# Raw first projections for two blocks, and the first block of x over two queues, in a two-layer convolutional decoder on eight cores

## The chip, the cores and the metric

One Trainium2 chip, 8 NeuronCores, one program launched on all of them. The metric is the device time in microseconds (us) of the slowest core. A program on all eight cores has a second, slower state in some executions, in which one die runs at a lower granted clock; only runs in the fast state are compared here. "Mean core span" below is the mean over the eight cores and over the fast runs of a kernel of the time from a core's first to its last instruction. It scatters less than the time, which one late core decides.

Engines: PE (TensorE), DVE (VectorE), ACT (ScalarE), POOL (GpSimd) and SP (SyncE, which issues loads). A **projection** in this text, as in the prediction, is one matmul of 128x128 weights by 128x512 (or 128x64) tokens; eight of them, one for each chunk k of the 1024 channels, make one output tile.

## The reference, cut to what matters

```python
def hybrid_layer(x, ...):                       # two layers
    h = rmsnorm(x, norm_g)                      # x * rsqrt(mean(x^2) + eps) * g
    p = h @ w_in                                # a, gate, z_A | B, C, hb, z_B
    u = a_val * sigmoid(a_gate);  v = gc * hb   # GLU; gated product
    ca = layernorm(causal_dwconv(u, ...))       # width 31, group A
    y_a = silu(ca) * silu(z_a)
    y_b = gb * causal_dwconv(v, ...) * silu(z_b)    # width 3, group B
    return x + concat(y_a, y_b) @ w_out
```

Each core has 2048 + 64 tokens, in four blocks of 512 and one of 64 (blocks 0 to 4).

## The kernel before: the parts that matter here

The kernel is written as a list of operations with their dependencies. Its own scheduler, a Python class that runs when the program is built, plays the operations through with assumed durations and load times, and thereby fixes the order of the instructions on every engine. Each engine then works its list off in that order, with semaphore waits.

```python
class Sched:
    def op(self, eng, fn, dur, reads=(), writes=(), chan=None, dma=0.0, pkt=0.1, lat=0.0, ..., urgent=False, name=""): ...
    def run(self):          # plays all ops; an op starts when its inputs are there BY THE ASSUMED TIMES
        ...                 # -> self.order[engine], the instruction order
    def emit(self, ...):    # puts out each engine's list in that order, with the waits it needs
```

The RMS statistic of a block: four pairs of squares on ACT, added in pairs on DVE, then one matmul with ones for each pair (a "statistic"), then Ln and Exp, then h = x * gain * rstd on DVE. (The last pair of block 0 goes to PE unsummed, as two matmuls.) While block 0's statistics come in, both kernels also put out **filling matmuls** of 128 columns ("warm" in the source), whose result nobody reads: 62 before, 60 after.

```python
def rms_stat(part, ...):
    for kp in range(4):
        act(Square, x[2kp], x[2kp+1] -> s)                      # 128x1024
        dve(s[:n] += s[n:2n])                                   # pair sum
        mm("stat", b, n, [(ones, s[:n])], urgent=True, ...)     # one 512-column matmul
    lo = act(Ln, b -> r);  ex = act(Exp(-0.5 * r) -> b)
def rms_apply(...): dve(h[k] = x[k] * gain[k] * b)              # eight times
```

The start: x of block 0 in four loads of 512 KB on the SP queue, the gain vector ("vecs", 28 KB) on the ACT queue, everything else on the POOL queue, in the order below. w1 to w4 are the weight slices of group A's first heads, w5 and w6 those of group B.

```python
    x_load(0)                                                      # SP, four loads
    S.op("act", dma vecs <- vecs_d, chan="c0", dma=0.2, pkt=0.02)  # gain vector
    ...                                                            # POOL: five memsets, then
    wA = [w_load(8), w_load(0), w_load(9), w_load(1)]              # w1..w4
    x_load(1, ("pool",))
    wB = [w_load(32), w_load(40)]                                  # w5, w6
    for q in (2, 3, 4): x_load(q, ("pool",))
```

## Time and profile before

| | before |
|---|---|
| time, fast runs | 1117.88 and 1116.79 us (a third run, 1326.98, was slow) |
| spans of the cores, profiled execution (1121.72 us) | 1113.4 to 1116.3 us, core 6 1120.2 |
| first projection, mean of the cores | 16.85 us |
| w5 lands, mean | 27.90 us |
| "mark" (first projection with weights from y_sb), mean | 83.70 us |
| span minus mark | 1031.0 to 1031.2 us on seven cores |

The rows read: until the mark the start decides, after it PE runs nearly without waits for 1031 us. The lines of the profile are shown in the prediction.

### The profile page before, as it was taken

To read this page: it belongs to the slowest core of one execution; us is meant where nothing else is said; L and a number is where in the kernel's file an instruction comes from. 1 tells how busy PE (TensorE), PEld (TensorE's weight loads), DVE (VectorE), ACT (ScalarE), POOL (GpSimd) and SP (SyncE) were. 2 spreads that over 40 slices of the span, in tenths; PEclk is the share of its full clock that TensorE was granted. 3 is DMA by queue.
4 is the path that set the end of the run, shared out by engine and by line. 5 is a ranking of instruction groups with operands and counts; after the bars stand their busy time and mean duration, and the time that the engine had idled before them with its cause. 6 is when DMAs were issued, how large, how long until landed. Compare 5 with 4: busy or idle time off the path is not lost.

```text
span 1120.2 us, 20967 instructions; the slowest of 8 cores (1113.4 to 1120.2 us)
## 1 busy us (share of the span) xinstructions
PE 1093.2 (98%) x7087; PEld 545.4 (49%) x7087; DVE 762.7 (68%) x1583; ACT 442.6 (40%) x705; POOL 254.6 (23%) x409
## 2 busy tenths in 40 slices
PE   5999899999999999999999999999999999999996
PEld 3445455454545455444444545545454454554545
DVE  3675756886785777744774577587668668874667
ACT  4652334234431435542442144342533134553354
POOL 7212222131201211113471112102211021110162
PEclk9999999999999999999999999999999999999998
DMA  9947488546643666651033746936655247565025
GB/s 219 237 79 139 66 149 152 110 82 108 117 80 51 121 110 113 95 128 20 1 40 57 162 97 112 178 72 121 114 97 94 49 92 130 91 99 121 2 104 207
DMA packets 178824, 117.98 MB, mean 105 GB/s; under 512 B 139168, under 2 KB 152352, under 8 KB 178656
## 3 DMA queue, kind: packets, MB, share of 16 engines
q0 software_dynamic: 34352, 54.97, 31.6%
q1 hardware_dynamic: 144224, 61.65, 22.4%
q8 instruction: 59, 0.97, 0.4%
q14 instruction: 45, 0.37, 0.1%
q10 hardware_dynamic: 144, 0.03, 0.0%
HBM read 132.24 MB, written 36.19 MB: 150 GB/s over the span
## 4 chain that ended last, share of the span: by engine, by line
PE 95%; DMA 1%; DVE 1%; POOL 1%; ACT 1%; issue 0%; DVEq 0%; ACTq 0%; POOLq 0%
PE psb L617 91%; PE psb L797 2%; PE psb L799 2%; DMA wsl<-w_in_r 1%; DVE x_sb L720 0%; POOL toep L1015 0%; ACT L694 0%; POOL wsl L584 0%; POOL x_sb L984 0%; POOL u_sb L1004 0%; DVE h_sb L720 0%; ACT L736 0%; ACT psb L700 0%; ACT tmp L694 0%; POOL up_sb L1013 0%
## 5 line engine op out<-in xcount | busy, mean ns | idle before, releaser
L617 PE MATMUL psb<-h_sb,wsl 128*128 128x512 bf16 (+1 forms) x4160 | 762.7, 343 | 4.6 <-DMA wsl<-w_in_r 2.6
L617 PEld LDWEIGHTS psb<-h_sb,wsl 128*128 128x128 bf16 x4160 | 347.2, 98 | 382.5 <-issue 11.6
L617 PE MATMUL psb<-y_sb,wsl 128*128 128x512 bf16 (+2 forms) x992 | 186.9, 336 | 0.2 <-DVE x_sb L943 0.2
L943 DVE TENSOR_TENSOR x_sb<-x_sb,psb 128x512 f32<-128x512 f32 (+2 forms) x248 | 137.3, 577 | 50.6 <-PE psb L617 49.4
L617 PEld LDWEIGHTS psb<-y_sb,wsl 128*128 128x128 bf16 x992 | 85.1, 98 | 87.2 <-issue 0.3
L584 POOL DMA_DIRECT2D wsl<-w_in_r x104 | 56.0, 546 | 287.0 <-PE psb L617 205.6
L924 DVE SCALAR_TENSOR_TENSOR tmp<-vbuf,cw_b_sb,tmp 128x512 f32<-128x512 bf16 (+1 forms) x160 | 102.9, 654 | 15.7 <-ACT tmp L921 6.9
L738 DVE SCALAR_TENSOR_TENSOR u_sb<-tmp,psb 128x512 bf16<-128x512 f32 (+1 forms) x80 | 47.3, 592 | 76.3 <-PE psb L617 68.4
L736 ACT ACTIVATE tmp<-psb 128x512 f32<-128x512 f32 (+1 forms) x80 | 41.3, 521 | 138.5 <-PE psb L617 121.3
L892 ACT ACTIVATE tmp<-psb 128x512 f32<-128x512 f32 (+1 forms) x80 | 41.4, 520 | 136.0 <-PE psb L617 131.5
L894 DVE TENSOR_TENSOR vbuf<-psb,tmp 128x512 bf16<-128x512 f32 (+1 forms) x80 | 47.3, 594 | 61.2 <-PE psb L617 57.9
L775 DVE COPY toep<-wt_sb 32x512 bf16<-32x512 bf16 x256 | 75.2, 295 | 18.8 <-DMA wt_sb<-wt_d 7.2
L675 ACT ACTIVATE tmp<-x_sb 128x1024 bf16<-128x1024 f32 (+2 forms) x63 | 52.3, 856 | 69.1 <-DVE x_sb L943 58.6
L804 DVE TENSOR_TENSOR big<-psb,cbt_sb 128x320 bf16<-128x320 f32 x128 | 62.4, 487 | 23.4 <-PE psb L799 18.6
L769 POOL DMA_DIRECT2D wt_sb<-wt_d x64 | 34.8, 545 | 187.2 <-DVE toep L775 94.5
L929 ACT ACTIVATE tmp<-psb 128x512 f32<-128x512 f32 (+1 forms) x80 | 41.0, 521 | 88.6 <-PE psb L617 79.9
L883 ACT ACTIVATE tmp<-psb 128x512 f32<-128x512 f32 (+1 forms) x80 | 40.1, 521 | 70.2 <-PE psb L617 66.2
L921 ACT ACTIVATE tmp<-vbuf,cw_b_sb 128x512 f32<-128x512 bf16 (+1 forms) x80 | 50.5, 642 | 42.0 <-DVE vbuf L894 38.8
L878 ACT ACTIVATE tmp<-big,vecs_sb 128x512 f32<-128x512 bf16 (+1 forms) x80 | 54.4, 729 | 31.7 <-DMA big<-scr_c 31.3
L720 DVE SCALAR_TENSOR_TENSOR h_sb<-x_sb,vecs_sb,psb 128x512 bf16<-128x512 f32 (+1 forms) x80 | 47.3, 648 | 17.4 <-ACT psb L700 17.4
L617 PE MATMUL psb<-h_sb,y_sb 128*128 128x512 bf16 (+1 forms) x320 | 58.9, 342 | 0.0
L931 DVE TENSOR_TENSOR tmp<-psb,tmp 128x512 f32<-128x512 f32 (+1 forms) x80 | 46.7, 594 | 17.5 <-PE psb L617 13.8
(80 smaller groups left out, 941.4 us busy)
## 6 DMA issues: line engine op xcount, KB each, us to landing
wsl<-w_in_r POOLq DMA_DIRECT2D x104, 256.0 KB, 5.9
scr_u<-u_sb SPq DMA_DIRECT2D x16, 768.0 KB, 6.2
up_sb<-scr_u SPq DMA_DIRECT2D x16, 768.0 KB, 6.4
scr_c<-big SPq DMA_DIRECT2D x16, 640.0 KB, 6.6
big<-scr_c SPq DMA_DIRECT2D x16, 640.0 KB, 5.1
wt_sb<-wt_d POOLq DMA_DIRECT2D x64, 128.0 KB, 3.7
x_sb<-x_d POOLq DMA_DIRECT2D x12, 512.0 KB, 20.2
wsl<-w_out_r POOLq DMA_DIRECT2D x24, 256.0 KB, 5.3
```

The source lines that it names most:

```text
L584: return e.dma_start(out=wsl[:, v.slot, :], in_=src)
L617: ins = e.matmul(bank(v, n), lhsT=l_(), rhs=r_(), start=(first and i == 0), stop=(last and i == len(pairs) - 1))
L675: act((lambda e, s=s, kp=kp: e.activation(out=tmph[:, s.slot, 0:2 * n].rearrange("p (k c) -> p k c", k=2), in_=x2(kp, part), func=AF.Square)),
L720: dve((lambda e, k=k, out=out: e.scalar_tensor_tensor(out=out, in0=xs(k, part), scalar=vecs[:, gcol0 + k:gcol0 + k + 1], in1=bank(r, n), o ...
L738: dve((lambda e: e.scalar_tensor_tensor(out=u_blk(ub, q), in0=b3(tm(th, n), q), scalar=1.0, in1=b3(bank(bv, n), q), op0=ALU.add, op1=ALU.m ...
L775: dve((lambda e, p=p, c=c: e.tensor_copy(toep[p, tp.slot, :].rearrange("p (m x) -> p m x", x=128)[:, :, 32 * c:32 * c + 32], wt_sb[p, w.sl ...
L804: dve((lambda e, b=b, v=v, bias=bias: e.tensor_tensor(out=big[:, co.slot, 4 * b:4 * b + 4, :], in0=banks[v.slot][:, 0:384].rearrange("p (g ...
L878: act((lambda e, s=s, q=q, n=n: e.activation(out=b3(tm(s, n), q), in_=c_blk(cn.slot, q), func=AF.Silu, scale=vecs[:, 16 + col:17 + col], b ...
L894: dve((lambda e: e.tensor_tensor(out=v_blk(q, 0), in0=b3(bank(bh, n), q), in1=b3(tm(th, n), q), op=ALU.mult)), n, [bh, th], [v_r[q]], name ...
L921: act((lambda e, a=a, q=q, n=n: e.activation(out=b3(tm(a, n), q), in_=v_blk(q, 0), func=AF.Copy, scale=cw_b[:, l, j, 2:3])), n, [v_r[q], c ...
L924: dve((lambda e, a=a, q=q, n=n, lag=lag: e.scalar_tensor_tensor(out=b3(tm(a, n), q), in0=v_blk(q, lag), scalar=cw_b[:, l, j, 2 - lag:3 - l ...
L943: dve((lambda e: e.tensor_tensor(out=xs(m, part), in0=xs(m, part), in1=bank(v, n), op=ALU.add)), n, [v, xr], [xr], name=f"x{q}.{m}")
```

## The change

Intent: blocks 0 and 1 are projected from x * gain, without waiting for the RMS statistic; the scale by token (rstd) is multiplied into the result in PSUM afterwards. h itself, which later heads need, is made later on ACT and POOL ("finishing"). Squares of blocks 0 to 3 go to PE without a pair sum, so a pair takes two statistic matmuls in place of one. x of block 0 is issued by SP and ACT in turn. The heads are interleaved a little differently, and the slack for loads is 3.5 in place of 4.25.

```diff
 ORDER = [
-    "b0 C0 Z0 P2 a1 b1 C1 P3 C2 P4 Z1 O4 ...
+    "C0 b0 Z0 P2 a1 b1 C1 P3 P4 Z1 C2 O4 ...
+DIRECT = (0, 1, 2, 3)
+START = "u0 u1 h0 t0 t1 w0 w1 w2 w3 x1 w4 w5 x2 x3 x4"
+RAW = (0, 1);  FINISH = {2: (0,), 3: (1,)};  WARM = (20, 20, 20, 0)
-SLACK, SLACK_DMA, SLACK_FIRST, QUIET = 1.5, 4.25, 2.0, 40.0
+SLACK, SLACK_DMA, SLACK_FIRST, QUIET = 1.5, 3.5, 2.0, 40.0
 def rms_stat(...):
+    if direct:                                  # both squares straight to PE
+        st = mm("stat", b, n, [(ones, s[i*n:(i+1)*n]) for i in range(2)], ..., urgent=True)
+        continue
+def raw_scale(q):  dve(h[k] = x[k] * gain[k])                        # eight times
+def raw_finish(q, rv):  act(t = x[k] * gain[k]);  pool(h[k] = t * rv)    # eight times each
 def p1_block(..., rv=None):
+    dve(psum_g *= rv);  ...  dve(psum_v *= rv)                       # if raw
 def pb_a_block(..., rv=None):
-    act(copy c)
+    act(copy c)  or, if raw,  dve(c = psum_c * rv^2)
-x_load(0)
+x_load(0, ("sp", "act"))                        # the gain vector is issued behind x
 S.op("act", dma vecs <- vecs_d, chan="c0", dma=0.2, pkt=0.02)
```
(cut to its core)

## The prediction

> **What bounds the kernel now.** I first read the spans of the cores. Seven of the eight take 1113.4 to 1116.3 us; core 6, which the page shows, takes 1120.2. No die is slower than the other, so this is the fast state. The page's busy times and TensorE's waits on core 6 come next:
>
> ```profile
> PE 1093.2 (98%) x7087; PEld 545.4 (49%) x7087; DVE 762.7 (68%) x1583; ACT 442.6 (40%) x705; POOL 254.6 (23%) x409
> PE psb L617 <- DVE tmp L677: 10.5, 7, 6.6
> PE psb L617 <- DVE big L819: 3.2, 1, 3.2
> PE psb L617 <- DMA wsl<-w_in_r: 2.6, 1, 2.6
> PE psb L617 <- DVE h_sb L720: 2.0, 3, 0.9
> ```
>
> TensorE (PE) is the bound. It waits 18.5 us in all, and the waits restricted to the first 60 us hold nearly all of it. The 6.6 us piece ends at 6.63 us, before any projection exists. The 3.2 us wait (at 127.5 to 130.7 us) is on core 6 alone: none of the other seven lists it. So only the start can give time. The chain of waits over the start of core 6 (start, us, what):
>
> ```profile
> 3.79 3.49 POOL toep L1015 x2
> 7.28 2.26 POOL wsl L584 x4
> 9.54 2.04 POOL x_sb L984 x4
> 11.58 16.61 DMA wsl<-w_in_r
> 28.32 14.16 PE psb L617 x58
> ```
>
> The chain hardly sees the RMSNorm of block 0. It runs through GpSimd's issue of loads and through one load: the fifth weight slice ("w5", first of group B), issued at 11.58 us and landed at 28.2. To see how far this sets the end I took the first projection that reads its weights from y_sb as a mark: by then the same 256 wide and 64 narrow projections are done on each core.
>
> ```profile
> L617 PE MATMUL psb<-h_sb,y_sb x320: 192/379/382, 82.2 to 652.0; 128*128 128x512 bf16 x128, 128*128 128x64 bf16 x32
> L617 PE MATMUL psb<-h_sb,y_sb x320: 192/379/382, 84.1 to 658.8; 128*128 128x512 bf16 x128, 128*128 128x64 bf16 x32
> ```
>
> These are cores 0 and 6: marks 82.2 and 84.1. In order of cores 0 to 7 the marks are 82.2, 85.0, 83.0, 85.1, 82.5, 84.8, 84.1, 83.0, and w5 (11.58 us plus its time to landing) lands at 26.8, 28.9, 27.3, 27.8, 27.4, 28.7, 28.2, 28.1. Mark minus w5 is 54.9 to 57.3, mean 55.8 us. Span minus mark is 1031.0 to 1031.2 us on seven cores (1036.1 on core 6, with its extra wait). So the kernel is **w5's landing (26.8 to 28.9) + 55.8 + 1031.2**, and the last term is PE at full pace. A time lies some 1.5 us over the slowest span (1121.72 for 1120.2); 1116.3 + 1.5 gives 1117.8, as in the fast runs.
>
> The last view is the clock, in stretches of 5 us on core 6:
>
> ```profile
> 25.00:30.00 5.00, 2.44 (x8) 0.75 (x9) 1.19 (x3) 4.10 (x6) 5.00 (x10) 0.79 1.02 254
> 30.00:35.00 5.00, 5.00 (x22) 2.07 (x21) 2.80 (x6) 2.92 (x5) 1.28 (x3) 0.87 0.99 344
> ```
>
> The last three columns are granted clock, DMA share, GB/s. The clock drops after the wait for w5, and the DMA engines are full. The missing clock times 5 us is 1.7 us on core 6, 3.4 on core 3, nothing on cores 4 and 7.
>
> **What the Trainium skill says.** (1) "TensorE: Matmul & The Clock Gate", Part 1: after an idle window of about 3.4 us the clock is halved until PE has been busy for one. The trace agrees: weight loads 0.43 us apart from 28.3 to 31.3 us, 0.216 later. (2) "DMA: Bandwidth & Descriptors", "Issuing engines are not separate DMA queues": loads from several engines share 16 DMA engines, a second issuer saves only issue time. The trace agrees so far: four x loads take 1.81 us to issue, but land at about 4.8, 7.4, 9.8 and 11.0, with the DMA share at 0.98 from 5 to 10 us. (3) "GPSIMD Engine Reference", Key points: GpSimd shares its SBUF interfaces with VectorE and contends with its two-port modes. No row here isolates it. (4) "ScalarE: Activation LUTs", "What ACT_TABLE_LOAD costs": 1283 ns per load; the trace has 1283.
>
> **The change part by part.** I count with the instruction order of both programs.
>
> *Raw block 0.* Projections no longer wait for squares, sum, Ln, Exp (h from 15.64 us, first projection at 16.65). They need a piece of x times the gain, one VectorE tensor-by-scalar (0.42 us for 128x512 f32, from the like row at L1043), and weights. But w1 to w4 land on core 6 at 13.2, 15.3, 16.7 and 18.6 (issue plus landing), and the new order asks for w1, w2, w3 at its first three projections and for w4 at the seventh. So PE starts 3 us sooner and does six projections by 18.6. Then come 26 of block 0, the first of block 1 and the statistics of block 1, paced by x of block 1 (20.4 to 24.4 us, plus a square of 1.06). All of this ends near 26.5, and the next projection waits for w5.
>
> *What is done when w5 lands.* Before: 30 projections. After: 34, plus all of block 1's statistics. That is the point: four projections, 4 x 0.2166 = 0.9 us, not the 3 us of the earlier start. (0.2166 is 41 projections from 31.26 to 40.14.)
>
> *From w5 to the mark.* Before: 226 wide projections and 9 wide statistics x 0.2166 = 50.9, plus 68 narrow x 0.029 = 2.0: 52.9; measured 55.8, so 2.9 us of waits and half clock. After, statistics feed both squares straight to PE, twice the matmuls: 222 + 16 = 238 x 0.2166 = 51.5 + 2.0 = 53.5. Block 1 has no rms chain in front of its projections, and block 2's (x landed 35.8 us, h estimated from 40) comes before PE needs it (28.2 + 70 x 0.2166 = 43.4). So the waits of 0.87 and 0.40 us on h should go. I leave 0.9 us for half clock on the slower cores: 54.4. Gain **1.4 us**.
>
> *Two queues for x.* The bytes ahead of w5 are the same and the DMA engines full. I allow w5 **0.5 us** sooner.
>
> *ScalarE, GpSimd, VectorE.* Added: 16 scaled copies on ScalarE x 0.72 (L712) = 11.5 us, 16 products on GpSimd x 1.30 (L717) = 20.9, and on VectorE 16 raw scalings x 0.42 = 6.7 and ten PSUM products (five a raw block) x 0.69 (L894) = 6.9. Gone from VectorE: 16 h products x 0.74 (L720) = 11.9 and 15 pair sums x 0.43 = 6.5, so it comes out 4.8 lighter. The finished h of block 0 is needed at the 184th projection (w5 + 149 x 0.2166 + 3.5 = about 63.5 us), of block 1 at the 217th (about 73). GpSimd can start at about 35 us, so 20.9 us end well before, if ScalarE (26.5 us busy of 40 between 30 and 70 us) makes room for 11.5 more.
>
> *Reordered heads, smaller DMA slack.* No saving: after the mark PE already runs without waits. Sum: -1.4 - 0.5 = about -1.9 us on a fast time of 1117.3.
>
> **The rivals.** *The start pays in full.* If x lands clearly sooner over two queues, weights and w5 follow by 2 us and more, and with block 1 raw some 4 us go: near 1113. For: x moves at only some 250 GB/s then, against 330 later. Against: engines already 0.98 busy. *A new wait behind the finishing work.* ScalarE at 38 of 40 us may hold up tanh or Ln, or GpSimd's products the halo copy, the next weight loads and the first convolution: PE would wait 2 to 5 us, time 1118 to 1121. Against: seven of eight cores have 5 us and more between the halo data's landing (91 on core 0) and its use. *Nothing,* if w5 lands as late and half clock stays: about 1117. *The new order after the mark* could bring waits such as core 6's 3.2 us, for one core is enough to set the time.
>
> **Range and chances.** Centre 1115.5 us (1117.3 - 1.9, rounded). Low 1111 holds the first rival with a lucky set of cores, high 1119 the second one at half strength. Two per cent would be 22 us, more than all the waits of PE together, so I give faster 0.01, within 2% 0.97, slower 0.02 (a wait in every round of heads).
>
> **What would show it right or wrong.** Right: the first projection near 13 to 14 us, a wait on w5 near 27 us still in PE's waits, the h waits gone, mark at w5 + 54 to 55, span minus mark again 1031. Wrong: w5 landing under 26 us (two queues help), mark minus w5 over 56 (new waits on VectorE, ScalarE or GpSimd rows of the finishing work), or span minus mark over 1033 (the reorder costs).

## The result, and the profile after

| | before | after | after, again |
|---|---|---|---|
| time, median | 1117.8 us (fast runs 1116.79 to 1117.88) | 1119.41 us (1118.25 to 1121.27) | 1120.12 us (fast runs 1117.98 to 1121.40) |
| ratio to before, 95% interval | | 1.0019 [0.9999, 1.0039] | 1.0013 [1.0001, 1.0026] |
| first projection, mean of the cores | 16.85 | 15.47 | 15.79 |
| w5 lands, mean | 27.90 | 27.26 | 26.99 |
| projections and wide statistics done when w5 lands, mean | 29.8 and 8.0 | 31.9 and 14.4 | 30.5 and 13.9 |
| mark, mean | 83.70 | 83.88 | 83.93 |
| span minus mark, undisturbed cores | 1031.2 | 1031.4 to 1031.6 | 1031.5 to 1031.6 |

A ratio is the mean time of one kernel's fast runs over that of the other's of the same rounds, so it is not quite the ratio of the medians. The prediction was 1115.5 us with a range of 1111 to 1119: the class (within 2%) was right, the time lies a little above the range and the sign of the small change is wrong. Counts of instructions by a point of time are taken from the trace's records, of which a few are missing.

The page of the changed kernel shows a span of 1116.8 us and nothing odd at this scale:

```profile
PE 1093.7 (98%) x7100; PEld 545.1 (49%) x7100; DVE 764.4 (68%) x1577; ACT 451.9 (40%) x719; POOL 275.9 (25%) x425
```

The added work on ACT (+9.3 us) and POOL (+21.3 us) is where it was expected; DVE has 1.7 us more in place of the 4.8 us less that the prediction gave (the page before was core 6, this is core 4). What PE waited for on core 6, the core that the prediction read (us in total, times, longest):

```profile
PE psb L623 <- ACT tmp L670: 9.7, 2, 8.7
PE psb L623 <- DMA wsl<-w_in_r: 2.0, 2, 1.6
PE psb L623 <- DVE tmp L678: 1.4, 2, 0.9
PE psb L623 <- DVE tmp L933: 0.7, 1, 0.7
```

The 8.7 us piece lies before any projection, as the 6.6 us piece did before. The 1.4 us for L678 lie after the mark. The waits on h are gone, as predicted (on seven of eight cores; core 3 has 0.26 and 0.54 us). New is 0.98 us for a square of block 2 (L670) and 0.7 us for the product that takes the place of a copy (L933). And the weight wait has another meaning: it is no longer for w5, but for w3 (1.63 us) and w4 (0.39 us), just after the first projections. The chain of waits of that core (start, us, what) says the same from the other end:

```profile
9.54 2.10 POOL x_sb L1025 x4
11.64 0.97 POOL wsl L590 x2
12.61 18.91 DMA x_sb<-x_d
...
31.60 1.06 ACT tmp L670
...
33.72 0.70 DVE tmp L933
```

Before, the long load in this chain was w5; now it is x of block 2 (issued at 12.61 us), then its square, then the product. So it is on cores 1, 2, 3 and 6, where the first square of block 2 starts 0.1 us after its x has landed. On cores 0, 4, 5 and 7 it starts 0.3 to 0.9 us after, straight behind a copy of the finishing work (L735). ScalarE on core 5, where that x landed at 30.50 us:

```profile
30.47 0.71 ACT L735 ACTIVATE big<-x_sb,vecs_sb 128x512 f32<-128x512 f32 x1
31.08 1.04 ACT L670 ACTIVATE tmp<-x_sb 128x1024 bf16<-128x1024 f32 x1
```

PE waits for this square for 0.60 to 0.61 us on these four cores, and for 0.96 to 1.12 us on the other four.

The marks answer to the two lines of the prediction for cores 0 and 6 (fourth figure; 311 of 320 records are there):

```profile
L623 PE MATMUL psb<-h_sb,y_sb x311: 193/379/382, 83.0 to 652.8; 128*128 128x512 bf16 x124, 128*128 128x64 bf16 x32
L623 PE MATMUL psb<-h_sb,y_sb x311: 192/379/382, 84.2 to 654.2; 128*128 128x512 bf16 x124, 128*128 128x64 bf16 x32
```

Core 0 went from 82.2 to 83.0, core 6 from 84.1 to 84.2. Finally the stretches of 5 us from 25 and 30 us on core 6 (PE, weight loads, DVE, ACT, POOL; then clock, DMA share, GB/s):

```profile
25.00:30.00 5.00, 5.00 (x25) 2.28 (x24) 2.74 (x6) 2.49 (x4) 3.91 (x8) 1.00 1.07 272
30.00:35.00 5.00, 3.23 (x15) 1.17 (x15) 1.98 (x4) 4.61 (x7) 3.49 (x6) 1.00 0.98 316
```

From 25 to 30 us PE gained, from 8 instructions to 25: the wait for w5 is gone. From 30 to 35 it lost, from 22 to 15. **The wait moved; it did not go.**

### The profile page after: what moved, and what is told of

Its sections match the earlier page's. It is cut to its first block, busy times and chain, and to the rows that moved or that the text cites. A ratio compares the mean times of both kernels' runs of the same rounds, so it can differ in the third digit from the quotient of the medians.

```text
span 1116.8 us, 21060 instructions; the slowest of 8 cores (1114.2 to 1116.8 us)
## 1 busy us (share of the span) xinstructions
PE 1093.7 (98%) x7100; PEld 545.1 (49%) x7100; DVE 764.4 (68%) x1577; ACT 451.9 (40%) x719; POOL 275.9 (25%) x425
## 4 chain that ended last, share of the span: by engine, by line
PE 96%; DMA 2%; POOL 1%; DVE 0%; ACT 0%; issue 0%; DVEq 0%; ACTq 0%; POOLq 0%
PE psb L623 92%; DMA x_sb<-x_d 2%; PE psb L835 2%; PE psb L837 2%; DVE x_sb L752 0%; POOL toep L1060 0%; POOL wsl L590 0%; POOL x_sb L1025 0%; POOL u_sb L1056 0%; ACT tmp L670 0%; POOL up_sb L1058 0%; DVE tmp L678 0%; DVEq L1159 0%; DVE x_sb L984 0%; DVEq L413 0%
## 5 line engine op out<-in xcount | busy, mean ns | idle before, releaser
L931 ACT ACTIVATE tmp<-psb 128x512 f32<-128x512 f32 (+1 forms) x78 | 40.2, 518 | 135.2 <-PE psb L623 131.5
L813 DVE COPY toep<-wt_sb 32x512 bf16<-32x512 bf16 x256 | 77.9, 305 | 15.9 <-DMA wt_sb<-wt_d 3.0
L769 ACT ACTIVATE tmp<-psb 128x512 f32<-128x512 f32 (+1 forms) x76 | 38.7, 517 | 114.3 <-PE psb L623 100.4
L970 ACT ACTIVATE tmp<-psb 128x512 f32<-128x512 f32 (+1 forms) x80 | 41.2, 521 | 104.1 <-PE psb L623 81.9
L670 ACT ACTIVATE tmp<-x_sb 128x1024 bf16<-128x1024 f32 (+2 forms) x64 | 53.5, 859 | 72.5 <-DVE x_sb L984 58.2
L962 ACT ACTIVATE tmp<-vbuf,cw_b_sb 128x512 f32<-128x512 bf16 (+1 forms) x80 | 50.4, 642 | 58.0 <-DVE vbuf L935 54.4
L921 ACT ACTIVATE tmp<-psb 128x512 f32<-128x512 f32 (+1 forms) x80 | 40.7, 521 | 74.8 <-PE psb L623 65.0
L922 DVE TENSOR_TENSOR y_sb<-tmp 128x512 bf16<-128x512 f32 (+1 forms) x70 | 41.2, 599 | 25.5 <-ACT tmp L921 25.0
```

The source lines that it names most:

```text
L670: act((lambda e, s=s, kp=kp: e.activation(out=tmph[:, s.slot, 0:2 * n].rearrange("p (k c) -> p k c", k=2), in_=x2(kp, part), func=AF.Square)),
L813: dve((lambda e, p=p, c=c: e.tensor_copy(toep[p, tp.slot, :].rearrange("p (m x) -> p m x", x=128)[:, :, 32 * c:32 * c + 32], wt_sb[p, w.sl ...
L962: act((lambda e, a=a, q=q, n=n: e.activation(out=b3(tm(a, n), q), in_=v_blk(q, 0), func=AF.Copy, scale=cw_b[:, l, j, 2:3])), n, [v_r[q], c ...
```

## The experiments

Eighteen runs were made. The figures of those that recur are in the table at the end of this section; the texts before it give the edit and what follows. "Core span +0.65" means the mean core span of the kernel minus that of the kernel before in the same call; the kernel before gave 1114.44 to 1114.80 in the five calls, so differences under 0.4 us say little. A mark comes from one profiled execution; four profiles with the same order at the start (the changed kernel twice, f1 and e3) have marks of 83.21 to 83.93.

### Is there a difference at all, and what does one part do?

**a0, the changed kernel again.** No edit.

> The changed kernel once more, unedited, in more rounds. It measures the size of the difference to be explained and how much start and mark differ between executions. If the change costs what the first timing said, the fast runs give a ratio of 1.001 to 1.003 (1118.5 to 1120.5 us). If that was chance, the interval holds 0.998, the 1115.5 us that were predicted. Mean mark of the cores 83.5 to 84.3 us, span minus mark 1031.3 to 1031.7.

Measured: ratio 1.0013 [1.0001, 1.0026], core span +0.65, mark 83.93. The change does cost a little over half a microsecond per core and somewhat more in the time, and not the gain of 1.9 us that was predicted.

**e1, block 0 of x on one queue again.**

```diff
-x_load(0, ("sp", "act"))
+x_load(0)
```

> Undoes one part: the first block of x goes out on the SyncE queue alone again; the gain vector is then not held up behind x on the ScalarE queue. Theory (the two queues bring x no sooner, and put the gain vector at 10.3 to 12.2 us, so that the raw scaling starts late): gain vector back near 5 us, first projection 13 to 14.5 us in place of 15.5, mark 0 to 1 us earlier. Rival (the two queues are what makes the start fast, x and with it w1 to w5 come later without them): w5 0.5 us later (27.7 in place of 27.3) and the mark 0.5 to 1 us later, time up by as much.

Measured: 1116.0 us, ratio 0.9980 [0.9967, 0.9992], core span -1.97, first projection 14.0, mark 80.92, with w5 at 26.86 us. One edited argument is worth 2.6 us of core span and gives nearly the predicted time. w5 is not later for it, against the rival. The mark moved by 3.0 us, where the theory allowed 1; still it looked like a proof of the theory that it was meant for (the gain vector held up behind x), but that was not so: see f1 and f2.

**e2, pair sums on DVE again for blocks 1 to 3.**

```diff
-DIRECT = (0, 1, 2, 3)
+DIRECT = (0,)
```

> Undoes one part: the statistics of blocks 1 to 3 add their pairs of squares on VectorE again, so 12 matmuls of 512 columns fewer stand before the mark (24 statistics in place of 36). Theory (PE is the limit from the first projection to the mark, so every added matmul is paid in full): mark 2 to 2.6 us earlier (12 x 0.2157 = 2.6), mean 81.3 to 81.9, time 1116.5 to 1117.5, ratio to the kernel before 0.998 to 0.9995. Rival (a load sets the mark: w5 at 27.3 or x of block 2 at 35 to 37 us): PE waits instead for the same loads, mark within 0.5 us of 83.9, time unchanged at 1119. One instruction waits more tightly here, because the check asked for it (ordering on one engine up to 24 instructions back in place of 8); neither theory gives that a cost above 0.2 us.

Measured: 1130.06 us, core span +12.0. Both theories missed by far. The scheduler answered with another order altogether: only 160 wide projections stand before the first y_sb weight, in place of 256, so this "mark" is not comparable, and PE waits on pair sums, weights and h (core 6, between 13 and 85 us):

```profile
PE psb L623 <- DVE tmp L678: 4.5, 5, 1.0
PE psb L623 <- DMA wsl<-w_in_r: 4.2, 3, 3.3
PE psb L623 <- DVE h_sb L752: 3.2, 1, 3.2
```

So e2 does not tell what 12 statistic matmuls cost; k1 was made for that. It was the first sign of how much hangs on the order.

**e3, the old interleaving of the heads and the old slack.**

```diff
-ORDER = [ "C0 b0 Z0 P2 ... ]         # as after
+ORDER = [ "b0 C0 Z0 P2 ... ]         # as before
-SLACK, SLACK_DMA, ... = 1.5, 3.5, ...
+SLACK, SLACK_DMA, ... = 1.5, 4.25, ...
```

> Undoes one part: the heads are interleaved in the old order again and the slack for loads is 4.25 again; the start is instruction for instruction that of the changed kernel. Theory (the reorder is no saving and costs little after the mark): mark unchanged within chance (83.4 to 84.4), span minus mark 1031.2 in place of 1031.5 on the undisturbed cores, time within 0.1% of the changed kernel. Rival (the reorder is what the change loses): span minus mark 1029 to 1030.5, time 1 to 2 us lower.

Measured: 1117.91 us, ratio 1.0004 [0.9988, 1.0019], core span +0.73, mark 83.42, span minus mark 1031.6 to 1031.8. The reorder is worth nothing either way. The added 0.3 us after the mark, which this theory put down to it, do not come from it; where they come from stays open.

**e8, two queues on the kernel before.**

```diff
-    x_load(0)
+    x_load(0, ("sp", "act"))
```

> Does one part alone on the kernel before: x of block 0 over two queues, the gain vector thereby behind x. The kernel before does not need the gain vector until its sum of squares is through (h from 15.6 us), so a gain vector at 11 to 12 us should cost nothing there. Theory: mark within 0.5 us of 83.7, time within 0.05% of before, w5 0 to 0.5 us earlier. Rival (two queues make x come sooner): first projection 1 us earlier, mark 0.5 to 1 us earlier. Second rival (two queues slow x down): the reverse.

Measured: 1118.77 us, ratio 1.0003 [0.9988, 1.0018], core span +0.50 (three fast runs), mark 83.13, first projection 17.27, w5 at 26.85 us, gain vector at 10.7 to 12.4 us. Mark and core span point in opposite directions by half a microsecond, so two queues show neither gain nor loss in a start that does not ask for the gain vector early.

**e4, no raw projections.**

```diff
-RAW = (0, 1);  FINISH = {2: (0,), 3: (1,)}
+RAW = ();  FINISH = {}
-rv = rms_stat(whole(0), raw=True, early=True, direct=0 in DIRECT)
-raw_scale(0)
+r0 = rms_stat(whole(0), early=True, direct=0 in DIRECT)
+rms_apply(0, whole(0), r0)
```

> Undoes the main part: no raw projections and no finishing work; block 0 and block 1 go through the RMSNorm first as before, but with the two queues, the new order of heads and every square straight to PE (36 statistics). What the raw start is worth by itself. Theory (raw projections take 1.4 us off the first projection and let PE be busy before w5, worth some 2 to 3 us, about what the 15 added statistics cost): first projection 16.5 to 17.5, mark 85 to 87, time 1119.5 to 1122. Rival (the raw start is worth nothing, or its finishing work costs what it brings): mark 83.4 to 84.4 as in the changed kernel.

Measured: 1119.07 us, core span +0.40, first projection 18.39, mark 83.41. The rival was right: in the changed kernel's setting the raw start is worth nothing. Without it PE starts 2.9 us later and still reaches the mark at the same time. (The scheduler laid this kernel out anew too, with block 1's statistics behind 10 to 25 projections. What the raw start is worth in a good order was not tried.)

### Is it the gain vector's place on its queue?

DVE's first raw scaling on core 6 of the changed kernel (start, us, what; in brackets the idle time before it and what ended that):

```profile
11.78 3.88 DVE L725 TENSOR_SCALAR h_sb<-x_sb,vecs_sb 128x512 bf16<-128x512 f32 x8 [10.29 <-DMA vecs_sb<-vecs]
```

x is there from 7.4 us on; the 28 KB gain vector, issued behind two 512 KB loads, lands at 10.3 to 12.2 us on the eight cores, before the change at 4.8 to 8.0. A tempting cause. Two kernels with an untouched instruction order test it, one way and the other.

**f1, the gain vector's load moved to the front of its queue**, after the order is fixed.

```diff
 def emit(...):
+    a = self.order["act"]
+    a.insert(0, a.pop([o.chan for o in a].index("c0")))
```

> The changed kernel with one instruction moved: the ScalarE queue issues the gain vector's load ahead of its two loads of x, in place of behind them. Every other instruction stays where it was on its engine (the two orders were compared), so this is the cost of the gain vector's place alone. Theory (it is what the prediction left out; raw scaling cannot start before 12 us): gain vector near 5 us, raw scaling from 7 to 8 us, first projection 13 to 14.5, mark 1.5 to 3 us earlier than 83.9, time 1116 to 1117.5. Rival (the one-queue run gained because the load on one queue is better and because its instruction order is another one): first projection earlier, but PE then waits for w2, w3, w4 in turn and gains under 0.7 us at the mark.

**f2, kernel e1 with the gain vector's load moved behind x on the SP queue**, after e1's order is fixed.

```diff
 def emit(...):                                  # on top of e1
+    a, b = self.order["act"], self.order["sp"]
+    v = a.pop([o.chan for o in a].index("c0"));  v.eng = "sp"
+    b.insert([o.chan for o in b].index("x03") + 1, v)
```

> The counterpart: the one-queue kernel (e1) in its own instruction order, but with the gain vector's load moved to the SyncE queue behind all four loads of x. Theory: gain vector lands at 11 to 13 us, first projection back at 15.5 to 17, mark back at 83 to 84.5 and the time at 1118 to 1120, as in the changed kernel. Rival (e1 is fast through its order of instructions or its single queue): mark stays within 0.7 us of 80.9, time near 1116.

The same line in f1 and, second, in f2, core 6:

```profile
7.04 0.91 DVE L729 TENSOR_SCALAR h_sb<-x_sb,vecs_sb 128x512 bf16<-128x512 f32 x2 [5.54 <-DMA vecs_sb<-vecs]
```
```profile
11.99 3.26 DVE L732 TENSOR_SCALAR h_sb<-x_sb,vecs_sb 128x512 bf16<-128x512 f32 x8 [10.49 <-DMA vecs_sb<-vecs]
```

Measured: f1 scales from 7 us on and is still slow (1118.61 us, core span +0.85, mark 83.21); f2 scales from 12 us on and is still fast (1115.64 us, core span -1.66, mark 80.98). **The theory fell on both sides.** What e1 and f2 share, and f1 does not, is the order of the instructions.

### Is it the order, or the loads?

**h1, e1's order with exactly the changed kernel's loads.**

```diff
 def emit(...):                                  # on top of e1
+    a, b = self.order["act"], self.order["sp"]
+    for k, c in enumerate(("x01", "x03")):      # 2nd and 4th load of x back to ACT, ahead of the gain vector
+        o = b.pop([o.chan for o in b].index(c));  o.eng = "act";  a.insert(k, o)
```

> The order of instructions of the one-queue kernel (e1), with exactly the loads of the changed kernel: x of block 0 over the SyncE and ScalarE queues in turn, the gain vector behind x. My first theory (the gain vector's place) has fallen: f1 moved it and won 0.7 us of mark, f2 delayed it and lost nothing. New theory: the cost lies in the order that the kernel's own scheduler lays out. Told of two queues, it takes x for earlier than it comes, and puts block 0's last statistics and 60 filling matmuls ahead of the first projection, asks for w2, w3, w4 at the second, third and seventh projection, and puts block 1's statistics behind the 17th projection in place of the 33rd. Then the loads themselves do no harm in the order of e1: mark 80.3 to 81.8, time 1115.3 to 1117. Rival (the two queues themselves, through their landings of 7.4 and 11.5 us in pairs, cost the 3 us): mark 83 to 84.5, time 1118 to 1120.

Measured: 1115.65 us, ratio 0.9978 [0.9965, 0.9991], core span -2.02, mark 80.80. One order with three arrangements of the loads (e1, f2, h1) gives core spans within 0.4 us of each other; the changed kernel's order with two arrangements (a0, f1) gives spans 2.3 us and more above them. So it is the order (of all five engines: h1 and the changed kernel differ on each, PE from its 7th operation on). The two kernels side by side, PE alone on core 6 (start, us, what; in brackets idle time and its end). First the changed kernel:

```profile
15.76 0.59 PE L623 MATMUL psb<-h_sb,wsl 128*128 128x512 bf16 x2
17.99 1.02 PE L623 MATMUL psb<-h_sb,wsl 128*128 128x512 bf16 x4 [1.63 <-DMA wsl<-w_in_r]
19.40 4.22 PE L623 MATMUL psb<-h_sb,wsl 128*128 128x512 bf16 x11 [0.39 <-DMA wsl<-w_in_r]
23.45 0.59 PE L623 MATMUL psb<-tmp,ones_s 128*128 128x512 bf16 x2
...
32.80 0.59 PE L623 MATMUL psb<-tmp,ones_s 128*128 128x512 bf16 x2 [0.98 <-ACT tmp L670]
```

Then h1, with the same loads:

```profile
15.15 1.24 PE L631 MATMUL psb<-h_sb,wsl 128*128 128x512 bf16 x5
16.23 0.59 PE L631 MATMUL psb<-tmp,ones_s 128*128 128x512 bf16 x2
16.66 6.21 PE L631 MATMUL psb<-h_sb,wsl 128*128 128x512 bf16 x28
22.89 0.59 PE L631 MATMUL psb<-tmp,ones_s 128*128 128x512 bf16 x2
...
33.18 0.59 PE L631 MATMUL psb<-tmp,ones_s 128*128 128x512 bf16 x2 [0.58 <-ACT tmp L678]
```

Both begin within 0.6 us of each other. The changed kernel asks for w2 at its second projection, w3 at its third and w4 at its seventh, waits on this core for w3 and w4, falls to half clock (11 projections take 4.22 us), and by 23.45 us has done 17 projections; h1 asks for w2, w3, w4 at its 7th, 10th and 18th, waits for none, and by 22.89 us has done 33. In the order (not the profile) this reads, as numbers of wide projections that stand ahead of each thing:

```
                    w2  w3  w4  w5   statistics of block 1   statistics of block 2
before               1   2  12  30   25 27 28 36             77 79 81 83
after (a0, f1)       1   2   6  34   17 22 28 32             47 57 59 63
e1, f2, h1           6   9  17  44   33 36 38 42             69 72 75 78
e6                   8  16  24  41   32 34 36 39             69 72 75 78
e5                   3   6  19  44   25 36 39 42             68 71 74 77
k2                   1   2  24  41   21 26 31 42             69 72 75 78
k3                   1   2   6  36   24 29 34 39             57 59 61 67
k4                   1   2  24  38   27 31 41 44             71 74 77 80
```

The Trainium skill, "PSUM — Partial Sum Buffer", section "Engine vs sequencer instructions", says that matmuls start and complete in program order; the statistics stand in the traces where the order has them (compared up to block 2, in the kernel before, the changed kernel, h1 and e6). So a matmul whose operand is late holds up all behind it, even those that could run. On core 5 x of block 1 landed at 22.04 us and its square was ready at 23.16; the statistic behind the 17th projection stopped PE there for 2.21 us, with 15 of block 0's 32 projections by w1 to w4 still to do.

**e6, gain vector first and block 0 by weight slices**, so that w2 to w4 are asked for after 8, 16 and 24 projections.

```diff
-    x_load(0, ("sp", "act"))
-    S.op("act", dma vecs <- vecs_d, ...)
+    S.op("act", dma vecs <- vecs_d, ...)
+    x_load(0, ("sp", "act"))
-            sp = KC if (l == 0 and q < 4) else 1
+            sp = KC if (l == 0 and 0 < q < 4) else 1
```
(here, and in e2, k4 and k5, an instruction also waits for those of its own engine up to 24 places back in place of 8, in g2 and g3 up to 12, which freedom from races asked for in these orders; what this costs by itself was not measured)

> Takes away two waits of the start: the gain vector is issued ahead of x, and block 0's projections run one weight slice at a time, so w2, w3 and w4 are asked for after 8, 16 and 24 projections in place of 1, 2 and 6. Theory (PE's time after its first projection is work, so a start that does more of it early moves the mark): PE is busy from 13 to 15 us without waits for w2 to w4, some 24 projections in place of 6 done by 19 us, no half clock there; mark 1.5 to 3 us earlier, at least if the wait does not come back at w5, which is now asked for after 41 projections. Rival (the mark hangs on w5 or on block 2's x): the time won is handed back as a wait for w5 near 27 us or for block 2's squares near 31 to 37 us, mark within 0.7 us of 83.9.

Measured: 1115.84 us, ratio 0.9978 [0.9966, 0.9991], core span -2.05, mark 81.02. It starts at 16.0 us, later than the changed kernel, and yet reaches the mark 2.9 us earlier, with no wait at all for w2 to w4. When PE starts matters less than what it finds behind its first projection.

### What misled the scheduler, and what do the parts of the order cost?

In the changed kernel the scheduler assumes the gain vector at 16.3 us (measured 10.3 to 12.2) because its formula gives a small load behind two large ones a small share; and x of block 1 from 19.7 us, x of block 2 from 28.8 us (first pieces measured at 20.2 to 22.0 and at 29.5 to 31.5 on the eight cores). In e1 it assumes the gain vector at 4.8 us (measured 4.8 to 7.5). Five more runs follow this up.

**e5, gain vector first in the source, everything laid out anew.**

```diff
-    x_load(0, ("sp", "act"))
     S.op("act", dma vecs <- vecs_d, ...)
+    x_load(0, ("sp", "act"))
```

> The changed kernel with two lines of source exchanged, so that the gain vector's load is issued ahead of x of block 0 on the ScalarE queue, and the scheduler lays out everything anew (f1 moved the same load and kept the order). Theory (the scheduler took the gain vector for landed at 16.3 us, the chip shows 10.3 to 13.2; on that it put off the projections and put block 1's statistics early): with the vector first its order is much like that of e1, block 1's statistics stand behind the 33rd projection or later, and mark is 80.3 to 81.8, mean core span 1112.5 to 1113.3, time 1115.3 to 1117. Rival (only the single queue leads the scheduler to a good order): mark 82.5 to 84.

Measured: 1117.83 us, core span +0.44, mark 83.38: the rival. Its start is better than the changed kernel's (34.2 projections by 25 us in place of 25.0) and is given back later. Core 6 waits for finished h from POOL, for which the changed kernel never waits:

```profile
PE psb L623 <- POOL h_sb L737: 1.1, 1, 1.1
```

**k2, k3 and k4, the changed kernel's loads with the scheduler told measured times**: the gain vector (k2), x of blocks 1 to 4 (k3), both (k4).

```diff
-... [vecs_r], chan="c0", dma=0.2, pkt=0.02)
+... [vecs_r], chan="c0", dma=0.2, pkt=0.02, lat=-4.8)          # k2, k4
-... pkt=0.172 if q < 4 else 0.09, after=after, name=f"x{q}")
+... pkt=0.172 if q < 4 else 0.09, lat=1.5 if q > 0 else 0.0, after=after, name=f"x{q}")   # k3, k4
```

> Loads exactly as in the changed kernel, two queues and the gain vector behind x. Only the scheduler's picture is corrected: it is told that the gain vector lands at 11.5 us in place of 16.3. Its new order asks for w4 after 24 projections in place of 6 and has block 1's statistics after 21, 26, 31 and 42 projections (17, 22, 28, 32 in the changed kernel), block 2's after 69 to 78 (47 to 63); block 0's statistics still stand ahead of the first projection. Theory (the order is the cause, and most of it lies in w2 to w4 and the early statistics): mark 81 to 82.3, mean core span 1112.8 to 1114. Rival (the gain of e1 lies in its start, where PE begins before the last statistics of block 0): mark 83 to 84, mean core span 1114.7 to 1115.6.

> Loads and gain vector exactly as in the changed kernel; only the scheduler is told that x of blocks 1 to 4 lands 1.5 us later than it thinks, about what the traces show. Its order keeps the start (w2, w3, w4 at the 2nd, 3rd and 7th projection), and puts block 1's statistics after 24, 29, 34 and 39 projections in place of 17 to 32, block 2's after 57 to 67 in place of 47 to 63. Theory (early statistics cost 1 to 2 us of waits, the early w2 to w4 another 1 to 2): mark 82 to 83.2, mean core span 1113.5 to 1114.7. Rival (the statistics' place is of no account): mark 83.4 to 84.4, mean core span 1115.1 to 1115.7. Second rival (it is all of it): mark 80.5 to 81.8.

> The changed kernel's loads; the scheduler is told both times, gain vector at 11.5 us and x of blocks 1 to 4 1.5 us later. Correcting one of them gave 0.6 to 1.3 us of mean core span (k2, k3), the order of e1 gives 2.7. Theory (the two wrong times are what makes the changed kernel's order bad): the two gains add up, mark 81.2 to 82.4, mean core span 1112.7 to 1113.7, time 1115.3 to 1117. Rival (every new order wins here and loses there, as e5 did with a wait of 1.3 us at 74 us; e1 came out well by chance): mark 82.5 to 83.6, mean core span 1114 to 1115.

Measured: k2 1117.32 us, core span -0.32, mark 82.74; k3 1117.99 us, +0.37, 83.16; k4 1118.12 us, -0.02, 83.21. Against the +0.65 us of a0 the gains are 1.0, 0.3 and 0.7 us: the two do not add up. In k3 the statistics wait for 0.7 us in place of 1.8 to 2.8, but PE then waits 1.4 us for the result of a tanh in its stead. In k4 (core 6) w5 and others take over:

```profile
PE psb L623 <- DMA wsl<-w_in_r: 1.4, 2, 1.2
PE psb L623 <- ACT tmp L670: 1.0, 1, 1.0
PE psb L623 <- DVE h_sb L752: 0.7, 1, 0.7
PE psb L623 <- DVE oat L784: 0.7, 1, 0.7
```

**k5, e1 with x told.**

```diff
 ... lat=1.5 if q > 0 else 0.0 ...               # as k3, on top of e1
```

> The one-queue kernel e1, its scheduler told that x of blocks 1 to 4 lands 1.5 us later than it thinks. A last try for a faster version, and a test whether better times make better orders. Theory (they do): mark at most 80.9, mean core span at most 1112.8. Rival (the quality of an order is not settled by these times): mark 81.5 to 83, mean core span 1113.3 to 1115.

Measured: 1116.77 us, core span -1.16, mark 81.43: a truer time made the order slightly worse. So the wrong times are not the whole reason for the bad order. Each order settles which of several late things PE meets first, and e1's settles it well; that this is more than chance was not shown.

**k1, half of the added statistic matmuls left out, order untouched.** Its output is wrong, which doesn't matter for the time.

```diff
-            for i, (l_, r_) in enumerate(pairs):
+            use = pairs[:1] if cls == "stat" and len(pairs) == 2 and kw["name"][2] in "123" else pairs
+            for i, (l_, r_) in enumerate(use):
```

> Wrong result on purpose: of the two statistic matmuls for each pair of squares in blocks 1 to 3 only the first is issued, 12 matmuls of 512 columns fewer, every other instruction in the place that it has in the changed kernel. Measures what the added statistics cost by themselves, which e2 could not tell, because its order became another one. Theory (PE is the limit and pays them in full): 12 x 0.2157 = 2.6 us off the mark (81.3), mean core span 1112.6 to 1113.2. Rival (PE waits for squares at these places anyway, so the second matmul is partly free): mark 82.3 to 83.5, mean core span 1113.8 to 1115.

Measured: mark 83.14, against 83.88 and 83.93: 12 matmuls that take 2.6 us by themselves give back 0.75 us (0.3 us against e3, which starts alike; 0.5 us in core span). Waits ahead of statistics rise to 4.1 us, mean of the cores, from 1.8 and 2.8 in the two profiles of the changed kernel. The added statistics are **mostly free in the changed kernel, because PE stands at these places anyway**. So PE's work alone was not the limit up to the mark.

### Candidates that did not beat e1

**g3, w5 and w6 ahead of x of block 1** (one queue, by weight slices):

```diff
-START = "u0 u1 h0 t0 t1 w0 w1 w2 w3 x1 w4 w5 x2 x3 x4"
+START = "u0 u1 h0 t0 t1 w0 w1 w2 w3 w4 w5 x1 x2 x3 x4"
```

> A candidate to beat both: one queue for x, block 0's projections one weight slice at a time, and w5 and w6 issued ahead of x of block 1. PE then has 48 projections of block 0 (10.4 us) before it needs anything of block 1. Theory (PE's time from the first projection on is work, if the order asks for things after they land): w5 near 21 us, x of block 1 some 1.5 us later (22.5 to 27), waits between first projection and 25 us near zero, mark 79.5 to 81, time 1114.5 to 1116. Rival (x of block 2 is the limit by then; it lands as late as before): mark 81 as in e6, the time won comes back as waits on squares of blocks 1 and 2.

**g2, one queue, by weight slices, old interleaving and slack** (edits as in e1, e6 and e3 together):

> One queue, block 0's projections one weight slice at a time, and the heads in the old order with the old slack of 4.25. Tells whether the new order of heads is worth anything with a good start. Theory (the reorder is worth nothing; e3 gave the same time as the changed kernel): mark as in e6 (80.5 to 81.5), span minus mark 1031.2 to 1031.9, time 1115 to 1116.5. Rival (with the faster start the old order makes PE wait for halo data or weights in the first heads): span minus mark over 1033.

Measured: g3 1117.68 us, core span -0.55, mark 82.38 (neither theory nor rival); w5 lands at 20.4 us, but x of block 1 at 23.4 to 25.1, and waits ahead of statistics rise to 3.0 us. Here the bytes moved ahead only moved the wait. g2 1116.49 us, core span -1.67, mark 82.21 (later than its theory), span minus mark 1031.3 to 1031.6, so the old heads do as well as the new; its start waits for statistics (3.3 us).

### The runs that recur, in one table

Means over the eight cores of the profiled execution, in us. "Stat" is waiting ahead of statistics after the first projection, "early" other waiting before 25 us, "late" other waiting after it and before the mark; half clock is not in them. Waits are counted from start to start of matmuls, less 0.2157 us for the matmul itself. e2, e3, e8, g2, g3 and k5 stand in the text above. Half clock between first projection and mark, counted as half of the time for which the granted clock was 0.50, is 1.5 us before, 0.85 and 0.2 in the two profiles of the changed kernel, and none in e1, h1 and e6.

| run | median | ratio to before [95%] | core span minus before | first | stat | early | late | mark |
|---|---|---|---|---|---|---|---|---|
| before | 1117.8 | 1 | 0 | 16.85 | 2.2 | 0.6 | 3.2 | 83.70 |
| after | 1119.41 | 1.0019 [0.9999, 1.0039] | | 15.47 | 1.8 | 2.3 | 1.1 | 83.88 |
| a0 after again | 1120.12 | 1.0013 [1.0001, 1.0026] | +0.65 | 15.79 | 2.8 | 1.6 | 1.0 | 83.93 |
| f1 vector moved | 1118.61 | 1.0009 [0.9997, 1.0022] | +0.85 | 15.65 | 2.0 | 1.9 | 0.9 | 83.21 |
| **e1 one queue** | 1116.00 | 0.9980 [0.9967, 0.9992] | -1.97 | 14.02 | 1.2 | 1.1 | 1.7 | 80.92 |
| **f2** e1, vector late | 1115.64 | 0.9979 [0.9965, 0.9992] | -1.66 | 14.16 | 1.3 | 1.3 | 1.3 | 80.98 |
| **h1** e1, after's loads | 1115.65 | 0.9978 [0.9965, 0.9991] | -2.02 | 15.38 | 1.1 | 0.2 | 1.3 | 80.80 |
| **e6** by slices | 1115.84 | 0.9978 [0.9966, 0.9991] | -2.05 | 16.00 | 1.5 | 0.0 | 0.9 | 81.02 |
| e5 vector first | 1117.83 | 1.0000 [0.9986, 1.0014] | +0.44 | 14.67 | 2.0 | 1.2 | 2.4 | 83.38 |
| k2 vector told | 1117.32 | 0.9996 [0.9982, 1.0011] | -0.32 | 15.97 | 2.0 | 0.9 | 1.5 | 82.74 |
| k3 x told | 1117.99 | 1.0002 [0.9989, 1.0016] | +0.37 | 15.61 | 0.7 | 2.0 | 2.0 | 83.16 |
| k4 both told | 1118.12 | 1.0001 [0.9987, 1.0014] | -0.02 | 15.63 | 1.0 | 1.3 | 2.5 | 83.21 |
| k1 fewer statistics | 1117.82 | 1.0001 [0.9985, 1.0017] | +0.19 | 15.60 | 4.1 | 1.9 | 1.1 | 83.14 |
| e4 no raw | 1119.07 | 1.0004 [0.9988, 1.0020] | +0.40 | 18.39 | 0.8 | 0.4 | 0.2 | 83.41 |

The four versions in bold beat both kernels by 0.2%, with intervals that exclude 1 against the kernel before (g2 does so by a hair, 0.9985 [0.9971, 0.9999]). Two things may be read off. The three kernels with e1's order differ in "first" by 1.4 us and agree in the mark. And against the changed kernel (and its repetition), h1 with the same loads and the same start saves 1.4 to 2.1 us of "early" and 0.7 to 1.7 us of "stat": that is the price of the order, kind by kind, with 0.2 to 0.85 us of half clock besides; "late" gives 0.2 to 0.3 us back.

## Why the prediction was wrong, point by point

- **The first projection, "near 13 to 14 us".** It came at 15.5 us. The prediction counted x and w1; it did not count that all of block 0's statistics and 60 filling matmuls (L1035) stand ahead of the first projection in PE's order, nor that the gain vector lands at 10.3 to 12.2 us. f1 shows that the second alone is worth nothing in core span (+0.85 against +0.65).
- **Two queues, w5 0.5 us sooner.** Right in number (0.64 us sooner, 0.9 in the repetition), but two queues are not shown to be why: on one queue w5 came at 26.87 (e1), 27.15 (f2) and 27.2 us (k5), as early as on two. The kernel before has one profiled execution, and what made its w5 late stays open. What the prediction quoted from "DMA: Bandwidth & Descriptors" fits: in the changed kernel x lands at 7.4 and 7.7, 11.4 and 11.2 us on core 6, its last piece no sooner than before (11.0).
- **34 projections and all 16 wide statistics done when w5 lands. This step failed first.** 31.9 and 14.4 were done, that is 46.3 in place of 50, so 0.8 us of work (3.7 x 0.2157) went over the line. "Paced by x of block 1" was seen; that PE would stand before block 1's statistics with projections of block 0 undone was not. A good order has 41.4 and 14.4 by then (h1), with the same loads.
- **From w5 to the mark, 54.4 us = 53.5 of work + 0.9 of half clock. This is the term that was mis-sized**: measured 83.88 - 27.26 = 56.6. Work left was (256 - 31.9 + 32 - 14.4) x 0.2157 + 2.0 = 54.1; the other 2.5 us are waits and half clock. The h waits went as predicted, but 0.7 us for L933 and 0.6 us and more for squares of block 2 came in their place. The prediction set block 2's h against its first projection (43.4 us), and not block 2's statistics, which the new order moves from behind 77 projections to behind 47, against the landing of block 2's x. It also named this as the sign of being wrong ("mark minus w5 over 56").
- **"The wait on w5 still in PE's waits"**: no. PE arrives after w5. The bound moved from w5 to block 2's first square, which waits for its x on four cores and for ScalarE on the other four (three and five in the repetition).
- **Finishing work on ACT and POOL is hidden**: right for POOL, whose finished h PE waits for only in e5 (1.1 us), and only in part for ACT. There (36.5 to 37.3 us busy of 40 on cores 0, 4 and 6, as foreseen) a copy stands ahead of block 2's first square on four cores; this is a piece of the second rival. No run took that copy away alone, so its cost at the mark is not shown.
- **VectorE 4.8 us lighter**: it was 1.1 to 3.4 us heavier, core by core. On core 4 a raw scaling took 0.53 us, not 0.42. The second cause was left open in the prediction ("No row here isolates it"): the same four small pair sums, before and after, on core 4:

```profile
L677 DVE TENSOR_TENSOR tmp<-tmp x4: 178/180/181, 63.0 to 63.3; 128x64 bf16<-128x64 bf16 x4
L678 DVE TENSOR_TENSOR tmp<-tmp x4: 179/1214/1312, 60.7 to 63.1; 128x64 bf16<-128x64 bf16 x4
```

  Each of the three that took 1.17 to 1.31 us ran while GpSimd worked on a product of the finishing work (L737). PE waited for such a sum once, 0.24 us on core 3.
- **The added statistics**: counted at full price. k1 shows that here the 12 of blocks 1 to 3 cost 0.3 to 0.8 us of their 2.6.
- **The reorder saves nothing**: right (e3). Span minus mark rose by 0.3 us; that was not foreseen and is not explained.
- **The size of the prize** was about right: the change with a good order takes 1.7 to 2.0 us off the core span (e1, f2, h1), the prediction said 1.9. In h1 the mark even comes 54.1 us after w5 (predicted 54.4), but by other parts, and so by luck: 55.8 in place of 50 matmuls done at w5, and 2.0 us of waits and half clock in place of 0.9. The error was to take the order that the program fixes as given and harmless. The list of instructions was at hand and showed the statistic at place 17, and x of block 1 landing from 20.4 us stood in the prediction itself.

Sum: predicted -1.4 (w5 to mark) - 0.5 (w5) = -1.9. Measured: +0.8 - 0.64 = +0.2 at the mark, +0.3 after it, so +0.5; a0's core span says +0.65. Of the miss of 2.4 us, 2.2 lie between w5 and the mark: the work not yet done when w5 lands, and the waits after it. What the time shows beyond that comes from the slowest core, which in the four runs of the first timing ended at 1116.4 to 1119.4 us.

Two readings in the prediction were too generous: of the 18.5 us of waits on core 6 the first 60 us hold 14.0, not nearly all; and the half clock there followed a wait of 2.56 us, so "the trace agrees" holds for the halving and its length, not for an idle window of 3.4 us (see the last section).

## What to carry to other kernels

When a program fixes the order of an in-order engine, an earlier start is worth only what the engine finds behind its first instruction: count, for each late operand, how many instructions that could run stand behind it, and compare with the times of landing. Test a suspected load by moving it with the order kept, and a suspected order by keeping it with the loads changed; a source edit that lets a scheduler lay out everything anew changes both, and a run that agrees with the theory (e1) then proves nothing. A matmul that stands next to a wait may be free, so take work away (k1) before pricing it.

## What the Trainium skill lacked or had wrong

- "PSUM — Partial Sum Buffer", section "Engine vs sequencer instructions", has the fact (matmuls start and complete in program order). No page draws the consequence: with the same loads, two instruction orders (the changed kernel's and h1's, on all engines) differed by 2.7 us in mean core span (+0.65 and -2.02 against the kernel before).
- "TensorE: Matmul & The Clock Gate", Part 1, ties the half clock to an idle window of about 3.4 us. On core 4 of the changed kernel two waits of 0.57 and 2.08 us were enough; PE was busy for 1.80 of the 4.30 us before 18.3 us, and the clock then stood at 0.50 for 3.4 us:

```profile
14.00:18.30 4.30, 1.80 (x18) 0.91 (x15) 2.10 (x5) 1.86 (x3) 3.43 (x7) 1.00 1.02 181
18.30:21.70 3.40, 3.24 (x8) 1.20 (x9) 0.70 (x2) 0.71 (x1) 0.00 (x0) 0.50 1.01 290
```

  On core 5 a single wait of 2.21 us was not followed by half clock. So a window mostly idle can do; where the line runs, these runs do not show. The kernel before, too, fell to half clock on core 6 with a wait of 2.56 us.
- "DMA: Bandwidth & Descriptors", section "Issuing engines are not separate DMA queues", says rightly that a second issuing engine saves only issue time. It gives no figure for a small load that then stands behind large ones: 28 KB behind two loads of 512 KB landed at 10.3 to 12.2 us, alone on its queue at 4.8 to 8.0.
- No page treats the difference between the time and the slowest core's span: 1.5 us for the kernel before and 1.9 for the changed kernel in the profiled executions.
